# Expert results written by row to a DRAM table and read back once, in place of one-hot products onto the tokens

## The chip, the cores and the metric

The kernel runs on one core of a Trainium2 chip, as one program in one launch. The metric is the device time of one execution in microseconds (us). Times of engines, lines and queues come from a profile of one execution; its own time stands beside the median of the timed runs further down.

## The reference, cut to what matters

Two blocks follow each other on 512 tokens of width 1024, all in float32. The first mixes a bidirectional gated recurrence with a gated spatial mixing; the second has pooling, sparse attention, an attention to 256 memory tokens, and then a mixture of 32 experts in 4 groups of 8. Only the last part is touched. A router picks for each token one group and in it the two best experts, and a weight (gate) for each:

```python
def hierarchical_moe(h, ...):            # h: 512 x 1024, normed
    g_sel = argmax(h @ wg_router + bg_router)            # one of 4 groups
    top_v, top_i = top_k(e_logits of that group, 2)      # two of its 8 experts
    top_w = softmax(top_v) * g_w
    gates = one_hot(g_sel) x (one_hot(top_i) * top_w)
    for g in range(4):
        a = einsum('nd,edf->nef', h, w_gate[g]); b = einsum('nd,edf->nef', h, w_up[g])
        hid = silu(a) * b * gates[:, g, :, None]
        out = out + einsum('nef,efd->nd', hid, w_down[g])
x = x + out
```

So each token receives the results of exactly two experts, 1024 choices in all. An expert has 1 MiB of gate weights, 1 MiB of up weights and 1 MiB of down weights.

## The kernel before

**The stages ahead of the experts.** The kernel first does the two blocks up to the attention to memory. The tokens' values, x, then stand in the tile `fx` (4 tiles of 128 tokens x 1024), and each of the four is also stored to DRAM as `x3d` (L1123). The router works tile by tile (`route`, `count`, `place`): it leaves for each token i and choice j an exact one-hot row over the 32 experts (`ohs`) and the place of the token among those of its expert. An expert has 64 places (`CAP`). Should one expert have more tokens, a loop behind a condition at the end works through the rest; no row of this profile is from it.

**The lists.** `R0` is the one-hot rows times the token's number less 1024 (`tk`, `NOTOK`). `lists_of` (L1213) multiplies it with the one-hot places on TensorE (PE), so that the PSUM tile `plist` holds, for each pair of experts in its column, the token number less 1024 at each of 2 x 64 places, and 0 where a place is empty. `tokens` (L1264) adds 1024 and gives the list as integers (`srci`) and as floats (`srcf`); an empty place gives 1024. `fetch_rows` (L1276) gathers a pair's 128 rows from `x3d` into one of three tiles `hg` with an indirect DMA from GpSimd's queue (POOL); numbers above 511 are left out.

**The loop over the 16 pairs.** Step r works on the experts 2r and 2r+1 together, 64 rows each (L1384). It issues the loads of its gate, up and down weights from SyncE's queue (SP); each goes as soon as its buffer is free, and there are buffers for three pairs (`PLACES`, L1007). `turn_rows` transposes the gathered rows on PE in two groups of four (L1286), `expert_up` scales them on VectorE (L1295), multiplies with gate and up weights in 32 matmuls (`pgu`, L1302), takes Silu on ScalarE (L1306) and the product with the gate on VectorE (L1307). `fetch_rows` for pair r+3 goes out once the rows of pair r are transposed. `expert_down` (L1310) transposes the hidden values (L1316), copies them (L1317), multiplies with the down weights in two halves of 512 columns (`pdn`, 16 matmuls, L1326), and splits each half into a rounded part and a rest (`yh` on ScalarE, L131; `yl` on VectorE, L132), so that a one-hot product keeps the precision.

**Putting the results onto the tokens.** `where` compares the token numbers 0 to 511 with the list on VectorE (L1333) and gives a one-hot matrix `put`, 128 places x 512 tokens. For each of 4 token tiles and 2 halves `add` multiplies it with `yh` (L1339) and `yl` (L1340) and adds the product to `fx` on VectorE (L1341): 16 matmuls and 8 adds per pair. Step r runs this for pair r-1, behind its own up matmuls. The last pair does it at once, and each finished piece of `fx` is stored to `out` (L1357).

**Buffers and order.** Tiles of one tag share a fixed number of buffers, and a new tile waits until an old one of the tag has been read for the last time. The tag `s4` has 8 buffers of 128 x 1024; the tiles `hg`, the scaled rows, `yh` and `yl` use it, and in earlier stages many others. PSUM has three buffers of the tag `mm` (here `pgu`, and half of the products onto the tokens) and three of `sm` (`pdn`, and the other half). Within an engine, instructions run in the order in which the framework's scheduler has put them when the program was built. It does not keep the order of the program text: it takes an instruction when, by its own estimates of durations, what it waits for is done, and among several the one that stands earlier in the text. Semaphores are set by the framework from the tiles that are read and written.

The functions that the diff touches:

Of the kernel before, what the change touches and what calls it, by code (L numbers as in the profile page):

```python
# [4 lines left out]
F32 = mybir.dt.float32  # L5
F32R = mybir.dt.float32r
BF = mybir.dt.bfloat16
I32 = mybir.dt.int32
U8 = mybir.dt.uint8
AF = mybir.ActivationFunctionType  # L10
OP = mybir.AluOpType
# [4 lines left out]
S = 512  # L16
D = 1024
NEG = -3.0e38
GONE = -3.3e38
NOTOK = 1024.0  # L20
# [29 lines left out]
def ap_of(t, off, dims):  # L50

    return bass.AP(tensor=t.tensor, offset=t.offset + off, ap=[t.ap[0]] + [list(d) for d in dims])
# [9 lines left out]
def program(tc, I, out, sb, ps, dr, dbg, upto):  # L62
    nc = tc.nc
# [5 lines left out]
    def c1(shape, name, dt=F32):  # L69
        return sb.tile(shape, dt, name=name)  # L70
# [7 lines left out]
    def s4(name, shape=(128, 2, 512), dt=F32):  # L78
        return sb.tile(list(shape), dt, name=name, tag="s4", bufs=8)
# [80 lines left out]
    def psm(name):  # L160
        return ps.tile([128, 512], F32, name=name, tag="sm", bufs=3)
# [55 lines left out]
    for d in range(2):  # L217
        nc.sync.dma_start(lraw[:, d, :], bass.AP(tensor=lbt.tensor, offset=lbt.offset + d * D,
                                                   ap=[[1, 128], [128, 8]]))
# [231 lines left out]
    for h in range(8):  # L451
        p = ptp(f"tya{h}")
# [48 lines left out]
            split(t, yb[0][:, g, :], yb[1][:, g, :])  # L501


    SC = float(128 ** -0.5)
    mmT = a16("mmT", F32R, (128, 2, 8, 256))
    mw = row_bc(I["mem_norm_2"], D, "mw")
# [13 lines left out]
    mh = rbf[:, 2].rearrange("p (i e) -> p i e", i=4)  # L520
    nc.vector.tensor_scalar(trib, iota, ctok[:, 0:1], None, OP.is_gt)
    nc.gpsimd.memset(oneb, 1.0)
    tk = c1([128, 4], "tk")
    nc.vector.tensor_scalar(tk, ctok, -NOTOK, None, OP.add)
    kvm = e8("kvm", (128, 2, 1024))
    kmT = kvm[:, 0].rearrange("p (h m) -> p h m", h=4)
    vm = kvm[:, 1].rearrange("p (i c) -> p i c", i=2)
# [78 lines left out]
    for ip in range(2):  # L606
        xt = [s4(f"xr{2 * ip + ii}", (128, D)) for ii in range(2)]
        for ii in range(2):
            i = 2 * ip + ii
# [540 lines left out]
    def route(i):  # L1150

        def top(src, k, b, name):

            m8 = sb.tile([128, 8], F32, name=f"{name}8_{i}", tag="m8", bufs=6)
            V_.max(m8, src)
            V_.tensor_copy(best[:, i, b, 0:k], m8[:, 0:k])
            rest = carve(src.shape[-1])
            V_.match_replace(rest, best[:, i, b, :], src, GONE)
            return rest

        gl = lg[:, i, 0:8]
        rest = top(gl, 1, 0, "grp")
        V_.tensor_tensor(rest, rest, gl, OP.is_equal)
        em = carve(32)
        V_.scalar_tensor_tensor(em.rearrange("p (g e) -> p g e", g=4), ap_of(rest, 0, [[1, 4], [0, 8]]), -1e30,
                                ap_of(lg, i * 40 + 8, [[8, 4], [1, 8]]), OP.mult, OP.add)
        rest2 = top(em, 2, 1, "ex")
        V_.tensor_tensor(mh[:, i, :], rest2, em, OP.not_equal)

        def gates():  # L1170
            V_.tensor_copy(best[:, i, 2, 0:1], best[:, i, 1, 0:1])
            rest1 = carve(32)
            V_.match_replace(rest1, best[:, i, 2, :], em, GONE)
            V_.tensor_tensor(ohs[:, 0, i, :], rest1, em, OP.not_equal)
            V_.tensor_tensor(ohs[:, 1, i, :], rest2, rest1, OP.not_equal)
            eg, g = carve(4), carve(4)
            gw, dv, g1, g2 = (g[:, c:c + 1] for c in range(4))
            V_.tensor_scalar(dv, best[:, i, 0, 0:1], -1.0, None, OP.mult)
            nc.scalar.activation(eg, gl[:, 0:4], AF.Exp, bias=dv, accum_out=gw)
            V_.tensor_tensor(dv, best[:, i, 1, 1:2], best[:, i, 1, 0:1], OP.subtract)  # L1180
            nc.scalar.activation(dv, dv, AF.Exp)
            V_.tensor_scalar(g1, dv, 1.0, gw, OP.add, OP.mult)
            V_.reciprocal(g1, g1)
            V_.tensor_tensor(g2, g1, dv, OP.mult)
            V_.tensor_scalar(R0[:, :, i, :], ohs[:, :, i, :], tk[:, i:i + 1], None, OP.mult)
            r = rs[:, i:i + 1]
            for j, gj in enumerate((g1, g2)):
                V_.tensor_scalar(R2[:, j, i, 0, :], ohs[:, j, i, :], gj, r, OP.mult, OP.mult)
            V_.tensor_scalar(R2[:, :, i, 1, :], ohs[:, :, i, :], r, None, OP.mult)
        return gates  # L1190
# [73 lines left out]
    def tokens(p, n, name):  # L1264

        src = sb.tile([128, n], I32, name=name + "_i", tag=name[:2] + "_i")
        V_.tensor_scalar(src, p, NOTOK, None, OP.add)
        e = sb.tile([128, n], F32, name=name + "_e", tag=name[:2] + "_e")
        V_.tensor_scalar(e, p, NOTOK, None, OP.add)
        return src, e  # L1270

    hg = [s4(f"hg{b}", (128, D)) for b in range(3)]
    for b in range(3):
        nc.gpsimd.memset(hg[b], 0.0)
# [32 lines left out]
        V_.scalar_tensor_tensor(sa, sa, gate, pg[:, 256:512], OP.mult, OP.mult)  # L1307
        return sh

    def expert_down(sh, ws, src, name, last=False):  # L1310

        m = 128 // len(ws)
        sa, hd = sh[:, 0:256], sh[:, 256:512].rearrange("p (f t) -> p f t", f=2)
        tp = ptp(f"thd{name}")
        for f in range(2):
            nc.tensor.transpose(tp[:, f * 128:(f + 1) * 128], ap_of(sa, f, [[2, 128]]), ident)  # L1316
        nc.scalar.activation(hd, tp[:, :256].rearrange("p (f t) -> p f t", f=2), AF.Copy)  # L1317
        yh, yl = s4(f"yh{name}", (128, D), F32R), s4(f"yl{name}", (128, D), F32R)
        put = []

        def down(half):
            hs = slice(half * 512, half * 512 + 512)
            po = psm(f"pdn{name}_{half}")
            for f in range(2):
                for a, (gu, dn) in enumerate(ws):
                    nc.tensor.matmul(po[m * a:m * a + m, :], hd[:, f, m * a:m * a + m], dn[f][:, hs],  # L1326
                                     start=f == 0, stop=f == 1)
            split(po, yh[:, hs], yl[:, hs])

        def where():  # L1330
            put.append(w2(f"put{name}", dt=F32R))
            for i in range(4):
                V_.tensor_scalar(put[0][:, i * 128:(i + 1) * 128], iota, float(128 * i), src, OP.add, OP.is_equal)  # L1333

        def add(i, half):
            p = (pmm if half else psm)(f"pad{name}_{i}_{half}")
            hs = slice(half * 512, half * 512 + 512)
            pi = put[0][:, i * 128:(i + 1) * 128]
            nc.tensor.matmul(p, pi, yh[:, hs], start=True, stop=False)  # L1339
            nc.tensor.matmul(p, pi, yl[:, hs], start=False, stop=True)  # L1340
            V_.tensor_tensor(fx[:, i, hs], fx[:, i, hs], p, OP.add)  # L1341

        def add_rows():
            where()
            for i in range(4):
                for half in range(2):
                    add(i, half)

        if last:
            where()  # L1350
            for half in range(2):
                down(half)
            for half in range(2):
                hs = slice(half * 512, half * 512 + 512)
                for i in range(4):
                    add(i, half)
                    nc.sync.dma_start(out[0, i * 128:(i + 1) * 128, hs], fx[:, i, hs])  # L1357
            return None
        for half in range(2):
            down(half)  # L1360
        return add_rows

    srci, srcf = tokens(plist[:, 0:16], 16, "lst")
    for r in range(1, 4):
        fetch_rows(hg[r % 3], srci[:, r:r + 1])
    grs = c1([128, 2, 16], "grs")
# [14 lines left out]
        V_.tensor_copy(nmi, nmx)  # L1381

    add_rows = None
    for r in range(16):  # L1384
        es, (gtags, dtags), last = (2 * r, 2 * r + 1), PLACES[r % 3], r == 15
        gu, fetch = [], []
        for e, tag in zip(es, gtags):
            if e < len(gus):
                gu.append(gus[e])
            else:  # L1390
                t, f = load_gu(e, str(e), tag, True)
                gu.append(t)
                fetch += f
        dn = []
        for x, tag in enumerate(dtags):
            d, f = load_dn(es if len(dtags) == 1 else es[x:x + 1], f"{r}_{x}", tag, True)
            dn += d
            fetch += f
        for f in fetch:
            f()  # L1400
        ws = list(zip(gu, dn))
        rows = turn_rows(hg[r % 3], f"{r}") if r else rows0
        sh = expert_up(rows, grs[:, 1, r:r + 1], grs[:, 0, r:r + 1], ws, f"{r}",
                       None if r else other_lists)
        if r and r + 3 < 16:
            fetch_rows(hg[r % 3], srci[:, r + 3:r + 4])
        if r:
            add_rows()
        add_rows = expert_down(sh, ws, srcf[:, r:r + 1], f"{r}", last)


    nval = nc.values_load(nmi[0:1, 0:1], min_val=0, max_val=S)
# [3 lines left out]
    with tc.If(nval > CAP):  # L1416
        with tc.For_i(0, 32, 1) as e:
# [6 lines left out]
            for j in range(2):  # L1424
                rx = sb.tile([128, 4, 3], F32, name=f"rx{j}v", tag=f"rx{j}")
                for c in range(2):
                    V_.tensor_tensor(t, R2[:, j, :, c, :], ap_of(sel, 0, [[0, 4], [1, 32]]), OP.mult)
                    V_.tensor_reduce(rx[:, :, 1 + c], t, AX.X, OP.add)
                V_.scalar_tensor_tensor(rx[:, :, 0], rx[:, :, 2], 0.0, tk, OP.is_gt, OP.mult)
                Rx.append(rx)  # L1430
            for rr in range(4):
                p = psm(f"plx{rr}")
# [35 lines left out]
```

## Time and profile before

| | us |
|---|---|
| median of 3 runs | 1338.7 (1338.12 to 1342.65) |
| the profiled execution | 1341.01 |
| its span | 1339.2 |
| PE busy | 1300.7 (97%) |
| VectorE (DVE) busy | 776.3 (58%) |
| ScalarE (ACT) busy | 494.1 (37%) |
| GpSimd (POOL) busy | 211.0 (16%) |

The profile shows one execution. The span is the time from its first to its last instruction; the execution's own time is 1.8 us more. PE is the matmuls and PEld the loads of their stationary operand; the ends of matmuls are modelled. L1302 is line 1302 of the kernel. A queue's name has a q behind it (SPq). The granted clock of PE is 1.00 at 2.4 GHz and 0.50 at 1.2 GHz.

### The profile page before, as it was taken

How to read it: one execution, taken by the hardware profiler on the slowest of the kernel's cores; microseconds unless marked ns; L12 is line 12 of the kernel's file. 1: busy time of each engine (PE TensorE's matmuls, PEld its weight loads, DVE VectorE, ACT ScalarE, POOL GpSimd, SP SyncE). 2: the span in 40 equal slices, each digit the busy share in tenths (PEclk: the TensorE clock that was granted, in tenths of full speed). 3: DMA queues.
4: the chain of work that ended last, by engine and by line, in shares of the span. 5: the costliest groups of instructions: out<-in, count | busy, mean ns of one | idle time of the engine just before them, and what ended most of it. 6: DMA issues, size and time to landing. Idle time of an engine off the chain costs nothing. (4 is left out here: it accounts for less than half of the span.)

```text
span 1339.2 us, 21242 instructions
## 1 busy us (share of the span) xinstructions
PE 1300.7 (97%) x8566; PEld 1031.3 (77%) x8566; DVE 776.3 (58%) x1457; ACT 494.1 (37%) x853; POOL 211.0 (16%) x255
## 2 busy tenths in 40 slices
PE   6999999999999999999999999889999999999997
PEld 5898989899988888888899878757898944444443
DVE  4568676666662345444556479993447735555555
ACT  4455464645432244333433334345535211111111
POOL 2203011030010000100012465342011110000000
PEclk9999999999999999999999999899999999999999
DMA  6332223222423433234542322222187579999951
GB/s 187 94 96 62 66 64 95 64 64 64 159 77 95 124 97 92 66 102 158 175 147 68 95 71 64 64 83 95 64 285 297 204 303 417 416 409 414 418 219 65
DMA packets 114454, 207.60 MB, mean 155 GB/s; under 512 B 14342, under 2 KB 93958, under 8 KB 103216
## 3 DMA queue, kind: packets, MB, share of 16 engines
q1 hardware_dynamic: 106096, 197.88, 41.6%
q10 hardware_dynamic: 6096, 4.47, 1.1%
q0 software_dynamic: 2160, 3.85, 0.8%
q8 instruction: 69, 1.13, 0.4%
q14 instruction: 33, 0.27, 0.1%
HBM read 201.81 MB, written 8.39 MB: 157 GB/s over the span
## 5 line engine op out<-in xcount | busy, mean ns | idle before, releaser
L1302 PE MATMUL pgu<-gu,hgT 128*64 128x512 f32 x512 | 113.7, 593 | 0.0
L1302 PEld LDWEIGHTS pgu<-gu,hgT 128*64 128x64 f32 x512 | 37.7, 137 | 71.2 <-issue 66.0
L353 ACT ACTIVATE qk<-G 128x512 f32<-128x512 f32 x112 | 69.1, 665 | 51.6 <-DVE G L343 51.6
L1341 DVE TENSOR_TENSOR fx<-fx,pad 128x512 f32<-128x512 f32 x128 | 77.9, 681 | 1.1 <-PE pad L1340 1.1
L1326 PE MATMUL pdn<-dn,sh 128*64 128x512 f32 x256 | 61.5, 604 | 0.0
L340 DVE TENSOR_TENSOR G<-G,T 128x512 f32<-128x512 f32 x56 | 39.2, 701 | 31.4 <-ACT qk L353 28.6
L1307 DVE SCALAR_TENSOR_TENSOR sh<-sh,grs,pgu 128x256 f32<-128x256 f32 x16 | 7.7, 481 | 80.7 <-ACT sh L1306 80.7
L1339 PE MATMUL pad<-yh,put 128*128 128x512 f32 x128 | 52.8, 416 | 0.9 <-DVE fx L1341 0.9
L1340 PE MATMUL pad<-yl,put 128*128 128x512 f32 x128 | 49.9, 394 | 0.0
L131 ACT ACTIVATE yh<-pdn 128x512 fp32r<-128x512 f32 x32 | 19.1, 597 | 73.8 <-PE pdn L1326 73.8
L1306 ACT ACTIVATE sh<-pgu,grs 128x256 f32<-128x256 f32 x16 | 7.6, 474 | 101.5 <-PE pgu L1302 101.5
L1277 POOL DMA_INDIRECT hg<-x3d,lst_i x15 | 15.1, 1008 | 184.1 <-PE thg L1286 171.3
L304 POOL TENSOR_TENSOR T<-T 128x512 f32<-128x512 f32 (+6 forms) x56 | 37.0, 660 | 42.6 <-DVE T L271 38.8
L153 PE MATMUL pi<-wi,hT_h 128*128 128x256 f32 x128 | 37.7, 295 | 3.3 <-ACT wi L131 1.7
L132 DVE TENSOR_TENSOR yl<-pdn,yh 128x512 fp32r<-128x512 f32 x32 | 22.1, 691 | 31.1 <-ACT yh L131 31.1
L343 DVE TENSOR_TENSOR G<-G,T 128x512 f32<-128x512 f32 x56 | 38.8, 693 | 0.0
L1339 PEld LDWEIGHTS pad<-yh,put 128*128 128x128 f32 x128 | 24.1, 188 | 18.6 <-issue 13.2
L154 PE MATMUL pi<-wi,hT_h 128*128 128x256 f32 x128 | 37.6, 294 | 0.0
L155 PE MATMUL pi<-wi,hT_l 128*128 128x256 f32 x128 | 37.2, 291 | 0.0
L153 PE MATMUL pv<-wv,hT_h 128*128 128x256 f32 x128 | 36.8, 288 | 0.0
L155 PE MATMUL pv<-wv,hT_l 128*128 128x256 f32 x128 | 36.7, 286 | 0.0
L154 PE MATMUL pv<-wv,hT_h 128*128 128x256 f32 x128 | 36.5, 286 | 0.0
(542 smaller groups left out, 4143.3 us busy)
## 6 DMA issues: line engine op xcount, KB each, us to landing
gu<-in_expert_w_gate SPq DMA_DIRECT2D x32, 1024.0 KB, 8.6
gu<-in_expert_w_up SPq DMA_DIRECT2D x32, 1024.0 KB, 13.3
dn<-in_expert_w_down SPq DMA_DIRECT2D x27, 1024.0 KB, 10.2
wo_r<-in_w_out SPq DMA_DIRECT2D x16, 512.0 KB, 3.6
wq_r<-in_w_in SPq DMA_DIRECT2D x12, 512.0 KB, 3.5
dn<-in_expert_w_down SPq DMA_DIRECT2D x10, 512.0 KB, 10.3
wi_r<-in_w_in SPq DMA_DIRECT2D x8, 512.0 KB, 3.6
wfb_r<-in_w_in SPq DMA_DIRECT2D x8, 512.0 KB, 3.6
```

What stands on the lines that cost most here:

```text
L153: nc.tensor.matmul(o, ah, bh, start=first, stop=False)
L154: nc.tensor.matmul(o, ah, bl, start=False, stop=False)
L155: nc.tensor.matmul(o, al, bh, start=False, stop=last)
L304: nc.gpsimd.tensor_tensor(ap_of(T, o, [[n2, 2], [1, n2]]), ap_of(T, a, [[sa, 2], [2, n2]]), ap_of(T, a + 1, [[sa, 2], [2, n2]]), OP.mult)
L340: nc.vector.tensor_tensor(ap_of(G, 0, [[512, 2], [2 * m, nb], [1, m]]), ap_of(G, 0, [[512, 2], [2 * m, nb], [1, m]]), ap_of(T, a + 1, [[sa ...
L343: nc.vector.tensor_tensor(ap_of(G, 1024 + m, [[512, 2], [2 * m, nb], [1, m]]), ap_of(G, 1024 + m, [[512, 2], [2 * m, nb], [1, m]]), ap_of( ...
L353: nc.scalar.activation(ap_of(qk, a * 512, [[2 * m, nb], [m, 2], [1, m]]), ap_of(G, a * 512, [[2 * m, nb], [1024 + m, 2], [1, m]]), AF.Copy)
L1302: nc.tensor.matmul(pg[m * a:m * a + m, :], hT_[:, k, m * a:m * a + m], ap_of(gu, k * 256, [[2048, 2], [1, 256]]), start=k == 0, stop=k == 7)
L1326: nc.tensor.matmul(po[m * a:m * a + m, :], hd[:, f, m * a:m * a + m], dn[f][:, hs], start=f == 0, stop=f == 1)
L1339: nc.tensor.matmul(p, pi, yh[:, hs], start=True, stop=False)
L1340: nc.tensor.matmul(p, pi, yl[:, hs], start=False, stop=True)
L1341: V_.tensor_tensor(fx[:, i, hs], fx[:, i, hs], p, OP.add)
```

## The change

For pairs 0 to 13 (`DIRECT = 14`), the result of a pair is copied out of PSUM as it is, half by ScalarE and half by VectorE, into a tile `yr`, and an indirect DMA from POOL's queue writes its 128 rows into a DRAM table `yd` of 1024 rows: row t for a token's first choice, 512 + t for its second. An empty place has row 1024, which is left out. After pair 13 the table is read back in eight loads of 128 x 1024 on SP's queue, and each is added to `fx` on VectorE. Pairs 14 and 15 are put onto the tokens as before; their rows of the table are not written, so the table is first filled with zeros, from a zeroed tile of tag `s4`, by one DMA of 4 MiB on ScalarE's queue (ACT), issued in the text behind the first block's gated mixing.

The lists now hold the row of the table, and the token is worked out from it: `tk` has a second set of columns with 512 added, `R0` is made in two steps in place of one, and `places` takes the place of `tokens` for the pairs.

```diff
+    yd = dr.tile([2 * S, D], F32, name="yd")
+    zero = s4("zero", (128, D))
+    nc.gpsimd.memset(zero, 0.0)
+    nc.scalar.dma_start(yd.rearrange("(i p) d -> p i d", p=128), ap_of(zero, 0, [[0, 8], [1, D]]))
...
-    tk = c1([128, 4], "tk")
-    nc.vector.tensor_scalar(tk, ctok, -NOTOK, None, OP.add)
+    tk = c1([128, 8], "tk")
+    nc.vector.tensor_scalar(tk[:, 0:4], ctok, -NOTOK, None, OP.add)
+    nc.vector.tensor_scalar(tk[:, 4:8], ctok, S - NOTOK, None, OP.add)
...
-            V_.tensor_scalar(R0[:, :, i, :], ohs[:, :, i, :], tk[:, i:i + 1], None, OP.mult)
+            for j in range(2):
+                V_.tensor_scalar(R0[:, j, i, :], ohs[:, j, i, :], tk[:, 4 * j + i:4 * j + i + 1], None, OP.mult)
...
+    def places(p, n):
+
+        row, rowf = c1([128, n], "row", I32), c1([128, n], "rowf")
+        V_.tensor_scalar(row, p, NOTOK, None, OP.add)
+        V_.tensor_scalar(rowf, p, NOTOK, None, OP.add)
+        src, e = c1([128, n], "srci", I32), c1([128, n], "srcf")
+        V_.tensor_scalar(e, rowf, float(S), -float(S), OP.is_ge, OP.mult)
+        V_.tensor_tensor(e, e, rowf, OP.add)
+        V_.tensor_copy(src, e)
+        return row, src, e
...
-    def expert_down(sh, ws, src, name, last=False):
+    def expert_down(sh, ws, src, name, last=False, row=None):
...
+        if row is not None:
+            yr = s4(f"yr{name}", (128, D))
+            for half in range(2):
+                hs = slice(half * 512, half * 512 + 512)
+                po = psm(f"pdn{name}_{half}")
+                for f in range(2):
+                    for a, (gu, dn) in enumerate(ws):
+                        nc.tensor.matmul(po[m * a:m * a + m, :], hd[:, f, m * a:m * a + m], dn[f][:, hs],
+                                         start=f == 0, stop=f == 1)
+                if half:
+                    V_.tensor_copy(yr[:, hs], po)
+                else:
+                    nc.scalar.activation(yr[:, hs], po, AF.Copy)
+            nc.gpsimd.indirect_dma_start(out=yd, out_offset=bass.IndirectOffsetOnAxis(ap=row, axis=0), in_=yr,
+                                         in_offset=None, bounds_check=2 * S - 1, oob_is_err=False)
+            return None
...
-    srci, srcf = tokens(plist[:, 0:16], 16, "lst")
+    row, srci, srcf = places(plist[:, 0:16], 16)
+
+    def results():
+
+        for i in range(4):
+            for j in range(2):
+                t = s4(f"yt{i}_{j}", (128, D))
+                nc.sync.dma_start(t, yd[j * S + i * 128:j * S + (i + 1) * 128, :])
+                V_.tensor_tensor(fx[:, i, :], fx[:, i, :], t, OP.add)
+
...
+    DIRECT = 14
...
-        if r:
+        if add_rows:
             add_rows()
-        add_rows = expert_down(sh, ws, srcf[:, r:r + 1], f"{r}", last)
+        add_rows = expert_down(sh, ws, srcf[:, r:r + 1], f"{r}", last, row[:, r:r + 1] if r < DIRECT else None)
+        if r == DIRECT - 1:
+            results()
```

## Rows read from the trace of the kernel before

**Rows 1.** The page: busy us and share of each engine; GB/s in 40 slices.
```profile
PE 1300.7 (97%) x8566; PEld 1031.3 (77%) x8566; DVE 776.3 (58%) x1457; ACT 494.1 (37%) x853; POOL 211.0 (16%) x255
...
GB/s 187 94 96 62 66 64 95 64 64 64 159 77 95 124 97 92 66 102 158 175 147 68 95 71 64 64 83 95 64 285 297 204 303 417 416 409 414 418 219 65
```
**Rows 2.** Stretches of 20 us: length, each engine's busy us, clock, DMA share, GB/s.
```profile
1260.00:1280.00 20.00, 20.00 (x96) 9.19 (x96) 11.54 (x23) 2.65 (x5) 0.99 (x1) 1.00 1.02 417
```
**Rows 3.** One period in order of time: start, us, engine, line, operation [idle before].
```profile
1249.14 7.04 PE L1302 MATMUL pgu<-gu,hgT 128*64 128x512 f32 x32
...
1256.11 0.50 PE L1339 MATMUL pad<-yh,put 128*128 128x512 f32 x1
...
1256.25 0.47 ACT L1306 ACTIVATE sh<-pgu,grs 128x256 f32<-128x256 f32 x1 [6.30 <-PE pgu L1302]
...
1259.00 0.39 PE L1316 MATMUL thd<-csq,sh 128*128 128x128 f32 x2
...
1259.59 0.48 PE L1339 MATMUL pad<-yh,put 128*128 128x512 f32 x1
...
1260.69 1.94 PE L1326 MATMUL pdn<-dn,sh 128*64 128x512 f32 x8
...
1264.96 7.04 PE L1302 MATMUL pgu<-gu,hgT 128*64 128x512 f32 x32
```
**Rows 4.** Groups from 960 us on: busy us, mean ns, idle before, releaser.
```profile
L1302 PE MATMUL pgu<-gu,hgT 128*64 128x512 f32 x512 | 113.7, 593 | 0.0
...
L131 ACT ACTIVATE yh<-pdn 128x512 fp32r<-128x512 f32 x32 | 19.1, 597 | 73.8 <-PE pdn L1326 73.8
...
L132 DVE TENSOR_TENSOR wxo<-wxo_r,wxo 128x1024 fp32r<-128x1024 f32 x4 | 4.8, 1220 | 0.3 <-ACT wxo L131 0.3
```
**Rows 5.** DMA from 1100 to 1290: a queue's packets and MB; issues, us to landing.
```profile
q0 software_dynamic: 1584, 2.71, 3.8%
...
hg<-x3d,lst_i POOLq DMA_INDIRECT x11, 8.3
```
**Rows 6.** SP's queue, pair 15's first load, in order of time.
```profile
1272.03 0.33 SPq L979 DMA_DIRECT2D gu<-in_expert_w_gate  x1
```
**Rows 7.** Short stretches, columns as in rows 2.
```profile
999.00:1000.00 1.00, 1.00 (x10) 1.00 (x10) 0.19 (x1) 0.00 (x0) 0.00 (x0) 1.00 1.06 442
...
1086.00:1088.00 2.00, 1.98 (x12) 1.07 (x14) 0.00 (x0) 0.38 (x1) 0.00 (x0) 1.00 0.98 414
...
1290.00:1292.00 2.00, 2.00 (x14) 1.72 (x12) 2.00 (x5) 0.38 (x1) 0.00 (x0) 1.00 0.15 61
```
**Rows 8.** The last two pairs in order of time, columns as in rows 3.
```profile
1304.15 0.48 DVE L1307 SCALAR_TENSOR_TENSOR sh<-sh,grs,pgu 128x256 f32<-128x256 f32 x1 [5.27 <-ACT sh L1306]
...
1312.38 7.04 PE L1302 MATMUL pgu<-gu,hgT 128*64 128x512 f32 x32
...
1323.46 3.65 PE L1326 MATMUL pdn<-dn,sh 128*64 128x512 f32 x16
...
1329.03 4.26 DVE L1341 TENSOR_TENSOR fx<-fx,pad 128x512 f32<-128x512 f32 x7
```
**Rows 9.** Stretches around a wait of PE, columns as in rows 2.
```profile
730.00:735.00 5.00, 2.80 (x21) 2.57 (x21) 5.00 (x11) 0.98 (x2) 2.19 (x3) 0.92 0.00 0
735.00:740.00 5.00, 5.00 (x35) 5.00 (x34) 1.31 (x3) 0.21 (x1) 1.29 (x1) 0.74 0.00 0
```
**Rows 10.** PE in order of time, the first matmul behind that wait.
```profile
733.81 0.77 PE L185 MATMUL tp_h2T_h<-csq,xr 128*128 128x128 f32 x4 [2.20 <-DVE h2T_l L132]
```
**Rows 11.** SP's queue in order of time, four places.
```profile
352.34 0.34 SPq L509 DMA_DIRECT2D mem<-in_mem  x1
...
989.57 3.62 SPq L941 DMA_DIRECT2D x2d<-xs  x2
...
1016.70 0.34 SPq L992 DMA_DIRECT2D dn<-in_expert_w_down  x1
...
1032.83 7.62 SPq L1123 DMA_DIRECT2D x3d<-fx  x2
```

More of the change, by code (lines that the diff above doesn't have):

```diff
@@ L1428, in program @@
                     V_.tensor_reduce(rx[:, :, 1 + c], t, AX.X, OP.add)
-                V_.scalar_tensor_tensor(rx[:, :, 0], rx[:, :, 2], 0.0, tk, OP.is_gt, OP.mult)
+                V_.scalar_tensor_tensor(rx[:, :, 0], rx[:, :, 2], 0.0, tk[:, 0:4], OP.is_gt, OP.mult)
                 Rx.append(rx)
```

## The prediction

> **What bounds the kernel now.** I read the page's first two parts, then the expert stage by stretches, one period of it in order of time, its groups and its DMAs, and then the end. "Pair r" is the step that runs experts 2r and 2r+1.
>
> The reader sees TensorE (PE) at 97% of the span, and late in the span five slices in which the core moves 409 to 418 GB/s [rows 1]. Stretch by stretch it is the same: from 1100 to 1280 us, nine stretches of 20 us, PE is busy 20.00 of 20 us and the DMA share is 1.00 to 1.02 [rows 2]. So two resources are full at once. Which one holds the other? The order of one period tells. The up matmuls of pair 11 start at 1249.14; at 1256.11 PE goes on with 12 matmuls of the write-back (L1339, L1340), with two transposes at 1259.00, four more write-back matmuls from 1259.59, the down matmuls from 1260.69, and the up matmuls of pair 12 at 1264.96 [rows 3]: 15.82 us. The groups show 0.0 idle before the up matmuls [rows 4], so no weights are waited for. The transfers, on the other hand, go out when PE frees a buffer: pair 15's gate and up weights from 1272.03, as the up matmuls of pair 12 end [rows 6]. All weight traffic is over at 1290 + 0.15 x 2 = 1290.3 [rows 7], while pair 15's up matmuls start only at 1312.38 [rows 8]. PE is the bound; weights lie ready more than a pair ahead. The DMA is full at the same time: a period carries 6.29 MB of weights (2 experts x 3 MiB) and a gather of 2.71 MB / 11 = 0.246 MB [rows 5], 6.54 MB, and at 415 GB/s that takes 15.8 us. It has no slack.
>
> **What the change removes.** For pairs 0 to 13: 16 write-back matmuls, 4 compares (L1333), 8 adds to fx (L1341), and of each of two splits the second half. ScalarE stands idle 73.8 us before the 32 splits alone [rows 4], and VectorE is busy 11.54 of 20 us [rows 2]; work saved there is worth nothing by itself. On PE the write-back takes 1259.00 - 1256.11 = 2.9 us and 1260.69 - 1259.59 = 1.1 us. What it covers now comes up: after the up matmuls the hidden values go through Silu (0.47 from 1256.25 on), a product, two transposes (0.39) and a copy before a down matmul can start, four steps of some 0.45 with short gaps, until about 1258.3. Now down starts 4.6 us after up ends; then about 2.2 us, into which the next pair's eight row transposes fit. So PE's own period becomes 15.8 - 2.4 = 13.4 us, at best 15.8 - 4.0 = 11.8 if the next up matmuls fill the gap. 14 pairs x 2.4 = 34 us is what PE alone would give.
>
> **What the DMA lets through.** Not that much, because pair 15's weights can't land earlier: the DMA has been full since 1086 [rows 7]. The end of the weights stays at 1290.3 and is pushed back by what the change adds. Each direct pair writes its rows to yd, as many as it gathered: 0.246 MB, 0.59 us at 417 GB/s. Thirteen such writes lie ahead of the last weights: 7.7 us, and the last weights land at 1298.0. No row shows an indirect write. From below it is 0: with stores of x2d issued among loads [rows 11], one stretch has 442 GB/s [rows 7], above the 417 of the expert stage. From above it is twice as much, if all 128 rows of yr travel: 15.5 us. I take 7.7, since the gather, the nearest row, moved only 60 of its 128 rows (0.246 MB of 4 KB rows).
>
> The Trainium skill ("DMA: Bandwidth & Descriptors", section "Issuing engines are not separate DMA queues") says that transfers from all engines run on the same 16 DMA engines and interleave; this speaks against the change, as POOL's writes take from SP's weights. That page's specifications give a ceiling of 435 GB/s; by it, instead of the 417 measured, the stage's bytes from 1086 on (204 us x 415 GB/s + 3.2 MB = 87.9 MB) would end at about 1288, an estimate from that page, 10 us before mine. The trace shows 415 to 417 held for 180 us, and the measurement decides.
>
> PE's lead, 1312.4 - (1290.3 - 5.0) = 27 us, is used up at 13.4 us per pair against 6.79 MB / 417 = 16.3 us: 27 / 2.9 = 9 pairs. From pair 9 or 10 on the weights set the pace, and PE waits up to 2.9 us per pair. Such a wait costs clock: after 2.20 us of idle before 733.81 [rows 10] the granted clock was 0.92 and 0.74 in the two stretches of 5 us [rows 9], that is 3.4 us at 1.2 instead of 2.4 GHz, 1.7 us of work lost. That fits into the wait until the last pair, where I count 2 us.
>
> **The end.** Pair 15's gate and up weights land one down load (2.1 MB, 5.0 us) before the last: 1293.0, against a use at 1312.38 now. From that use to the end are 26.8 us [rows 8]; with nothing else late the span would be 1293.0 + 26.8 = 1319.8. But what is late next is the reading back. yd's reads wait for pair 13's write: its weights land around 1267, down ends about 1275, and a gather took 8.3 us from issue to landing in this stage [rows 5], so the reads go out at about 1284, on SP, behind all weights issued there before (pair 15's go out as pair 12 ends). 8 x 0.52 MB = 4.2 MB at 417 GB/s: they land from 1299.3 to 1308.1. Each is then added to fx, 128x1024 on VectorE; the nearest rows are 1.22 us (the split of wxo, that shape) [rows 4] and 2 x 0.61 (two adds of 128x512, 4.26 / 7) [rows 8]. The last such add ends at 1309.3. fx is one chain: pair 14's eight adds (4.9 us) come after these, pair 15's after those. PE is held too: pair 14's eight products sit in six PSUM buffers until their adds go, and pair 15's down matmuls need three of the same. I put these at 1309.3 + 6 x 0.61 = 1313.0. From there to the end are 1339.2 - 1323.46 = 15.7 us now [rows 8]: 1328.7. With 2 us for the clock, 1330.7. VectorE's own chain is shorter: 1309.3 + 2 x 4.9 + 1.4 (two splits) + 5.9 (from the last add, 1333.3, to the end) = 1326.4.
>
> **Small edits.** The memset and the 4.2 MB of zeros on ACT's queue need a buffer of tag s4. Loads that stand near them in the program went out as soon as such a buffer came free, mem at 352.34 [rows 11], so the fill falls there: 10 us of DMA beside a chunk of projection weights. If that chunk is late, its split waits on ScalarE, and Silu's and Sigmoid's like behind it in that queue, and then PE for PSUM. Between 0 and 5 us; I take 0, as mem shows that loads there have slack. The three extra VectorE steps in places (0.2 each) delay the first gathers by 0.6 us; the extra steps on tk lie beside PE. A write's issue on POOL is one step more between gathers 15.8 us apart; who waits behind it there is only the next gather, three pairs ahead of its use.
>
> The profiled execution took 1341.0 with a span of 1339.2, and lies 2.3 above the median of 1338.7. A span of 1330.7 is 1330.2 on the median's scale: 1330.
>
> **Rivals.**
> A, read-back hidden: reads or adds don't hold fx, and the end is 26.8 us behind pair 15's weights: 1319.8, on the median 1319. For it: writes might be free; against it: the reads queue behind the weights.
> B, nothing gained: writes cost the upper bound, weights end at 1305.8, and all that follows moves by 7.8: 1338. For it: a DMA that is full already; against it: the gather's 60 rows.
> C, slower, by a wait in VectorE's queue. That engine works in order, and the order is fixed beforehand by the framework's scheduler from its own estimates, not by program order: weights of pair 2 went out at 1016.70, ahead of x3d's stores at 1032.83, which stand before them in the program [rows 11]. If it believes that the reads land soon, their eight adds stand in the queue ahead of pair 14's product L1307, and pairs 14 and 15 wait for them: from that L1307 (1304.15) to the end are 35.0 us [rows 8]; from 1309.3 on that gives 1344. It decides as soon as that L1307 stands behind the last of these adds. Against it: the reads depend on pair 13's last step, which is late by any estimate.
> D, clock: PE, waiting in every pair, stays at 1.2 GHz. Its 13.4 us become 26.8, above 16.3, and from pair 10 on 5 x 10 us are lost: 1370 or more. Against it: 32 up matmuls in a row follow each wait, and after 733.81 the clock came back under such work.
>
> **Numbers.** Forecast 0.42 (its own range 1325 to 1336), A 0.18, B 0.18, C 0.15, D 0.07. This kernel's measurement tells 0.5%, 6.7 us, from no change: below 1332.0 is faster, above 1345.4 slower. Faster: A, and 0.75 of the forecast, 0.50. Slower: D, and C or B with anything late beside them, 0.21. Within: 0.29. The range 1316 to 1347 leaves out D, the late side of C and the early side of A.
>
> **What would show it.** Right: no L1339 before pair 14; DMA share 1.0 to about 1298; from pair 9 or 10 on PE idle before pgu, released by DMA, at some 16.3 us per pair, the granted clock below 1.00 there; eight adds of 128x1024 between 1299 and 1310 with DMA as their releaser. Wrong: no DMA wait before pgu (PE's own period is above 16.3), traffic that ends well off 1298 (the price of a write), reads that land among the weights, or pair 14's product after 1305 behind the new adds (C).

## The result and the profile after

The changed kernel takes 1352.15 us (median of five runs, 1350.01 to 1357.38) against 1338.7 of the kernel before (five runs, 1336.12 to 1342.65): 1.0106 times as long, 95% interval [1.0072, 1.0139]. It is slower by 13 us, where 1330.0 was forecast and 1316 to 1347 allowed. The profiled execution took 1357.1, 5 above its median; its span of 1355.1 is 15.9 us longer than the 1339.2 of before.

Three lines of its page, the engines, the GB/s and POOL's DMA queue (packets, MB), answer [rows 1]:
```profile
PE 1260.5 (93%) x8342; PEld 994.9 (73%) x8342; DVE 700.7 (52%) x1291; ACT 486.0 (36%) x839; POOL 227.8 (17%) x270
...
GB/s 184 94 95 63 64 63 95 63 69 58 267 121 90 97 94 94 89 113 196 145 128 41 119 61 42 94 113 61 83 371 177 240 407 419 417 417 419 416 238 64
...
q0 software_dynamic: 4176, 7.47, 1.5%
```
PE does 40 us less work and yet the span grows. The core moves over 405 GB/s in six slices, in five before. Four stretches, columns as in [rows 2], say where the time lies:
```profile
1100.00:1120.00 20.00, 18.86 (x92) 6.99 (x90) 3.80 (x6) 2.05 (x4) 4.08 (x4) 1.00 1.02 423
...
1260.00:1280.00 20.00, 16.50 (x70) 5.76 (x64) 2.37 (x4) 2.05 (x4) 2.41 (x3) 0.91 1.01 415
1280.00:1300.00 20.00, 1.19 (x8) 0.52 (x4) 0.69 (x1) 0.00 (x0) 1.95 (x2) 0.66 0.82 338
1300.00:1320.00 20.00, 7.41 (x25) 2.91 (x27) 10.91 (x10) 0.00 (x0) 0.00 (x0) 0.57 0.57 218
```
Up to 1280 it is as forecast: DMA share 1.01 to 1.02, PE with gaps (16.50 of 20 us, where [rows 2] had 20.00). Then PE all but stands still for a whole stretch (1.19 of 20 us). The same place in order of time, with POOL's last writes, SP's reads, VectorE and PE:
```profile
1285.52 0.98 POOL L1351 DMA_INDIRECT yd<-yr,row  x1 [7.70 <-DMA yd<-yr,row]
1294.25 0.97 POOL L1351 DMA_INDIRECT yd<-yr,row  x1 [7.75 <-DMA yd<-yr,row]
1302.08 8.80 SPq L1406 DMA_DIRECT2D yt<-yd  x8
1305.74 1.23 DVE L1407 TENSOR_TENSOR fx<-fx,yt 128x1024 f32<-128x1024 f32 x1 [24.46 <-DMA yt<-yd]
...
1309.30 2.51 DVE L1407 TENSOR_TENSOR fx<-fx,yt 128x1024 f32<-128x1024 f32 x2 [0.37 <-DMA yt<-yd]
1311.85 1.29 DVE L1314 TENSOR_TENSOR hgT<-thg,ffc 128x512 f32<-128x512 f32 x2
1312.60 9.31 PE L1321 MATMUL pgu<-gu,hgT 128*64 128x512 f32 x32 [31.41 <-DVE hgT L1314]
1313.06 4.87 DVE L1407 TENSOR_TENSOR fx<-fx,yt 128x1024 f32<-128x1024 f32 x4
...
1322.52 0.48 DVE L1326 SCALAR_TENSOR_TENSOR sh<-sh,grs,pgu 128x256 f32<-128x256 f32 x1 [4.59 <-ACT sh L1325]
```
Read it from the matmuls of 1312.60 upwards. They are pair 14's up matmuls, and they waited 31.41 us for hgT, the turned rows of pair 14. VectorE writes these at 1311.85, right behind four of the eight result adds, and the first of these had waited for the read-back. The reads (L1406) go out at 1302.08, 7.8 us after the last write to yd. Pair 14's product stands at 1322.52, against 1304.15 in [rows 8]: 18.4 later. From there to the end are 32.6 us, 2.4 fewer than the 35.0 of before, since pair 13 has no write-back left behind it. 18.4 - 2.4 = 16.0: the whole loss lies in this one wait and, with 2.3 us, in the slower matmuls behind it (9.31 us against the 7.04 of [rows 3]).

POOL's queue in order of time, gathers (L1296) and writes (L1351), shows why the last write is so late:
```profile
1130.47 1.02 POOL L1296 DMA_INDIRECT hg<-x3d,srci  x1 [11.07 <-PE thg L1305]
1143.87 1.00 POOL L1296 DMA_INDIRECT hg<-x3d,srci  x1 [12.39 <-PE thg L1305]
1157.34 0.98 POOL L1296 DMA_INDIRECT hg<-x3d,srci  x1 [12.46 <-DVE yr L1348]
1158.63 1.02 POOL L1351 DMA_INDIRECT yd<-yr,row  x1 [0.30 <-issue]
...
1248.07 1.00 POOL L1351 DMA_INDIRECT yd<-yr,row  x1 [0.31 <-issue]
1259.46 1.01 POOL L1351 DMA_INDIRECT yd<-yr,row  x1 [10.39 <-DMA yd<-yr,row]
```
Every write goes to the same table, so each waits for the landing of the one before, and where three gathers stand ahead of a write in the queue (1130 to 1158) it also waits for them. Behind the last gather five writes were left over; they go out 8.6 to 11.4 us apart, from 1259.46 to 1294.25, although pair 13's rows were in yr at 1281.3.

### The profile page after: what moved, and what is told of

The parts are those of the page before. It is cut to its first block, busy times and chain, and to the rows that moved or that the text cites. A ratio compares the mean times of both kernels' runs of the same rounds, so it can differ in the third digit from the quotient of the medians.

```text
span 1355.1 us, 20558 instructions
## 1 busy us (share of the span) xinstructions
PE 1260.5 (93%) x8342; PEld 994.9 (73%) x8342; DVE 700.7 (52%) x1291; ACT 486.0 (36%) x839; POOL 227.8 (17%) x270
## 3 DMA queue, kind: packets, MB, share of 16 engines
q0 software_dynamic: 4176, 7.47, 1.5%
## 5 line engine op out<-in xcount | busy, mean ns | idle before, releaser
L1321 PE MATMUL pgu<-gu,hgT 128*64 128x512 f32 x512 | 123.3, 611 | 41.0 <-DVE hgT L1314 36.0
L1345 PE MATMUL pdn<-dn,sh 128*64 128x512 f32 x224 | 51.2, 598 | 0.3
L1296 POOL DMA_INDIRECT hg<-x3d,srci x15 | 15.4, 1028 | 157.7 <-DVE yr L1348 109.5
L1348 DVE COPY yr<-pdn 128x512 f32<-128x512 f32 x14 | 9.7, 692 | 54.3 <-PE pdn L1345 54.3
L154 PE MATMUL pg<-wga,hT_h 128*128 128x256 f32 x128 | 36.5, 285 | 0.0
L153 PE MATMUL pg<-wga,hT_h 128*128 128x256 f32 x128 | 36.4, 285 | 0.0
L155 PE MATMUL pg<-wga,hT_l 128*128 128x256 f32 x128 | 36.2, 283 | 0.0
L1345 PEld LDWEIGHTS pdn<-dn,sh 128*64 128x64 f32 x224 | 14.8, 136 | 27.0 <-issue 24.0
L319 PE MATMUL pl<-qk 128*64 128x64 f32 x896 | 34.3, 225 | 0.0
```

The costliest lines, as they stand in the source:

```text
L153: nc.tensor.matmul(o, ah, bh, start=first, stop=False)
L154: nc.tensor.matmul(o, ah, bl, start=False, stop=False)
L155: nc.tensor.matmul(o, al, bh, start=False, stop=last)
L319: nc.tensor.matmul(p[64 * j:64 * j + 64, c * 64:c * 64 + 64], kt[:, k0:k0 + 64], qt[:, q0:q0 + 64], start=True, stop=True)
L1296: nc.gpsimd.indirect_dma_start(out=h, out_offset=None, in_=x3d, in_offset=bass.IndirectOffsetOnAxis(ap=sidx, axis=0), bounds_check=S - 1, ...
L1321: nc.tensor.matmul(pg[m * a:m * a + m, :], hT_[:, k, m * a:m * a + m], ap_of(gu, k * 256, [[2048, 2], [1, 256]]), start=k == 0, stop=k == 7)
```

## The theories

BUFFERS. yr, yt, hgT, hg, yh and yl come from one set of eight buffers (tag s4). Three hold the gathered rows, and the other five are handed round in program order. There the eight read-back tiles stand ahead of pair 14's turned rows: they take the five buffers, then three of these again, and the turned rows, ninth in the row, get the buffer of the fourth tile, which the fourth add frees. So they wait for the table. (The trace fits: five reads go out from 1302.08 to 1304.7, the other three at 1307.00, 1308.96 and 1310.56, each as one of the first three adds ends, and hgT follows the end of the fourth.) The rivals: ORDER, the adds stand ahead of pair 14 in VectorE's queue by the scheduler's choice alone, which is the prediction's rival C one step earlier; BANDWIDTH, the written bytes take the DMA from the weights; and CHAIN, the loss is that the reads are dated by the row of writes.

## The experiments

**Six pairs instead of 14** (`DIRECT = 6`, read-back behind pair 5).

> Six pairs instead of 14 are written to the table, and the read-back is asked for after pair 5; 3.0 MB instead of 7.2 MB of writes. BUFFERS: pair 6's turned rows wait for the fourth result add in the same way, and these for the read-back behind the last write of the chain: pair 6's up matmuls start near 1193 instead of 1157, the ten pairs left take the 15.8 us of the kernel before, and the time is 1350 to 1368, at 1360: no better than with 14 pairs, although under half is written. BANDWIDTH: the loss goes with the volume written and the gain with the pairs; 1325 to 1335. ORDER: as BUFFERS, since adds and turned rows stand in the same order in VectorE's queue.

Measured: 1364.1 us, ratio 1.0203 [1.0186, 1.0220]. The wait of pair 6, in order of time:
```profile
1174.57 0.97 POOL L1351 DMA_INDIRECT yd<-yr,row  x1 [7.80 <-DMA yd<-yr,row]
1181.88 7.86 SPq L1406 DMA_DIRECT2D yt<-yd  x8
1185.55 3.84 DVE L1407 TENSOR_TENSOR fx<-fx,yt 128x1024 f32<-128x1024 f32 x3 [32.53 <-DMA yt<-yd]
1189.55 1.23 DVE L1407 TENSOR_TENSOR fx<-fx,yt 128x1024 f32<-128x1024 f32 x1
1190.81 1.29 DVE L1314 TENSOR_TENSOR hgT<-thg,ffc 128x512 f32<-128x512 f32 x2
1191.55 8.76 PE L1321 MATMUL pgu<-gu,hgT 128*64 128x512 f32 x32 [38.65 <-DVE hgT L1314]
```
Again four adds, then the turned rows, then the up matmuls, 1.5 us off the expected 1193. (A write moves 0.259 MB, as shown below, so both volumes in the expectation, 3.0 and 7.2 MB, are about twice too high; their proportion stands.) With under half the writes the kernel is slower still: BANDWIDTH is out as the main cause. ORDER isn't yet.

**The adds asked for last**, in the same eight buffers:
```
-        if r == DIRECT - 1:
+        if r == 15:            # ahead of expert_down, behind pair 14's add_rows
             results()
```


> The read-back is asked for in the program after pair 14's results have been put back, in pair 15, in the same eight buffers. BUFFERS: the turned rows of pairs 14 and 15 get their buffers first, up matmuls of pair 14 near 1283 and of pair 15 near 1297; the reads still go out near 1302 because the last write lands then (chain of writes), the adds run from 1306, and with the sixteen put-back adds of pairs 14 and 15 around them VectorE ends near 1330: 1332 us (1327 to 1337). ORDER: the same. BANDWIDTH: above 1342. If the chain of writes is not what dates the reads, they go out near 1290 and the time comes to 1322 to 1326.

Measured: 1332.58 us, 0.9967 [0.9950, 0.9984], the expected figure and a little faster than before. Pair 14's up matmuls start at 1275.78, pair 15's at 1293.14, the reads at 1297.51:
```profile
1275.78 1.07 PE L1321 MATMUL pgu<-gu,hgT 128*64 128x512 f32 x2 [0.75 <-DVE hgT L1314]
...
1293.14 7.55 PE L1321 MATMUL pgu<-gu,hgT 128*64 128x512 f32 x32
...
1297.51 12.80 SPq L1406 DMA_DIRECT2D yt<-yd  x8
```
ORDER allows it too.

**The read-back's own buffers**, asked for ahead of pair 14's work as in the change:
```
-                t = s4(f"yt{i}_{j}", (128, D))
+                t = yts[i // 2][:, 2 * (i % 2) + j, :]    # one tile of tag w16, one of a16
```
(`results()` moves behind the requests for pair 14's weights, so that these keep their buffers.)

> The eight tiles of the read-back are taken from two tiles of other tags (the freed weight buffer of pair 13's down part and one 16 KB weight buffer), no longer from the eight buffers that the row tiles, the turned rows and the result rows share; the reads and adds still stand ahead of pair 14's work in the program. Theory BUFFERS (pair 14's turned rows get the buffer that the fourth result add frees, and so its up matmuls wait for the whole read-back): pair 14's up matmuls start at 1283 +- 3 us instead of 1312.6; its product then stands behind two result adds in VectorE's queue and ends near 1308 instead of 1322, and the run takes 1338 us (1334 to 1343). Rival ORDER (the adds stand ahead of pair 14 in VectorE's queue for their own sake): pair 14's up matmuls still start after 1305 and the time stays within 3 us of 1352. Rival BANDWIDTH (the 7 MB of writes take the DMA engines from the weights, and that is the loss): unchanged within 3 us of 1352, the up matmuls waiting for weights.

Measured: 1350.93 us, 1.0092 [1.0075, 1.0109]: the time of the rivals, with the start of BUFFERS.
```profile
1279.47 1.07 PE L1321 MATMUL pgu<-gu,hgT 128*64 128x512 f32 x2
...
1282.55 8.69 PE L1321 MATMUL pgu<-gu,hgT 128*64 128x512 f32 x30 [2.00 <-DMA gu<-in_expert_w_up]
...
1297.20 1.75 SPq L1407 DMA_DIRECT2D ytw<-yd  x4
...
1301.87 0.44 SPq L986 DMA_DIRECT2D gu<-in_expert_w_gate  x1
...
1321.81 9.54 PE L1321 MATMUL pgu<-gu,hgT 128*64 128x512 f32 x30 [2.99 <-DMA gu<-in_expert_w_up]
```
Pair 14's up matmuls run 30 us earlier (the first two start at 1279.47), but my edit put the reads on SP's queue ahead of pair 15's weights. The queue works in order, the reads waited for the last write until 1297.20, and the weights behind them went out from 1301.87, 27 to 31 us later than in the changed kernel; pair 15's up matmuls wait for them, 30 of the 32 until 1321.81. One wait was exchanged for another, so I took that one away as well: the same kernel with `nc.gpsimd.dma_start` for the reads.

> The run with own buffers for the read-back once more, with the eight reads sent from POOL's queue behind the last write instead of from SP's, where they stood ahead of pair 15's last weights (these went out at 1301.9 to 1306.6 and pair 15's up matmuls waited for them until 1321.8). BUFFERS: pair 14's up matmuls near 1283 again; one or two result adds stand ahead of pair 14's rests, so pair 15's up matmuls start near 1308, the other adds run beside them, and the end comes 26.8 us later: 1336 us (1332 to 1341). Rival ORDER or BANDWIDTH: 1348 or more, as in the run before it.

Measured: 1337.03 us, 0.9989 [0.9973, 1.0006].
```profile
1281.18 7.05 PE L1321 MATMUL pgu<-gu,hgT 128*64 128x512 f32 x30 [1.50 <-DMA gu<-in_expert_w_up]
...
1301.53 2.21 POOL L1407 DMA_DIRECT2D ytw<-yd  x4 [7.29 <-DMA yd<-yr,row]
...
1305.21 1.23 DVE L1408 TENSOR_TENSOR fx<-fx,ytw 128x1024 f32<-128x1024 f32 x1 [15.89 <-DMA ytw<-yd]
1306.35 0.68 DVE L132 TENSOR_TENSOR yl<-pdn,yh 128x512 fp32r<-128x512 f32 x1
1306.95 1.28 DVE L1314 TENSOR_TENSOR hgT<-thg,ffc 128x512 f32<-128x512 f32 x2
1307.69 9.47 PE L1321 MATMUL pgu<-gu,hgT 128*64 128x512 f32 x32 [13.04 <-DVE hgT L1314]
```
The reads go out at 1301.53, as late as in the changed kernel, and pair 14 no longer cares; 1352.15 - 1337.03 = 15.1 us are what the shared buffers cost (15.7 by the two ratios; the move to POOL's queue, which was to undo the wait of the run before, is in it). With other buffers the scheduler itself puts pair 14's turned rows ahead of the adds, although these are still asked for first, so for pair 14 the order was a consequence of the buffers and not the cause. What is left of ORDER is in the last four lines: one result add, which waits for the table, stands ahead of pair 14's last split and pair 15's turned rows, and PE waits 13.04 us.

**Two tables by turns**, the odd pairs' read back and the results of the even pairs left out:
```
-            nc.gpsimd.indirect_dma_start(out=yd, ...
+            nc.gpsimd.indirect_dma_start(out=yds[int(name) % 2], ...
```


> As the changed kernel, but the pairs write by turns into two tables, and only the table of the odd pairs is read back (left out: the results of the even pairs; both tables are filled with zeros first). A write now waits for the write two pairs back. Theory CHAIN (the reads are dated by the writes going one after another, each behind the landing of the one before): the last write goes out soon after its rows are ready at 1281, the reads near 1291 instead of 1302, pair 14's up matmuls start near 1303 instead of 1312.6, and the time is 1343 us (1340 to 1347). Rival (the reads are dated by the weights ahead of them on SP's queue, or by the gathers ahead of the writes on POOL's): reads out at 1298 or later, and the time 1349 to 1353.

Measured: 1355.3 us, 1.0123 [1.0106, 1.0140]. A miss, and not for the rival's reason either.
```profile
1283.74 0.98 POOL L1352 DMA_INDIRECT yd<-yr,row  x1 [17.61 <-DVE yr L1349]
1291.95 17.22 SPq L1407 DMA_DIRECT2D yt<-yd  x8
1305.12 5.05 DVE L1408 TENSOR_TENSOR fx<-fx,yt 128x1024 f32<-128x1024 f32 x4 [22.13 <-DMA yt<-yd]
```
The last write and the reads go out 10 us earlier, as expected. But the first add starts at 1305.12, where it was 1305.74: the reads now run behind the weights still in flight and take 14.2 us to land (median) instead of 5.7. CHAIN dates the reads' issue and is worth nothing here. The likely reason is that the DMA has no room for them until 1300 (share 0.90 to 1.03 in every 2 us from 1290 on); why they need another 5 us after that, no run shows.

**No read-back, and neither read-back nor writes** (`results()` left out; then the write in `expert_down` as well).

> Left out: the eight reads of the table and the eight adds, so the output lacks the results of 14 pairs; all writes stay. BUFFERS: pair 14 waits for nothing late, pair 15's up matmuls start when its weights have landed, near 1297, and the end follows 26.8 us later as in both kernels: 1325.7 us (1321 to 1331), below the kernel before. ORDER says the same. BANDWIDTH: the writes alone hold the weights up, so the time stays above 1342.

> Left out: all writes to the table and its read-back, so the output lacks the results of 14 pairs. Set against the run without read-back alone (1324.8 us) it prices the writes. Pair 15's up matmuls wait there for weights until 1295.5. By the 0.59 us a pair that the prediction charged the weights for a write, 14 writes give 8 us back: 1316.5 us. By the full time of 0.52 MB at 420 GB/s, 1.25 us each, they give 17.5 us back: 1307 us, and TensorE's own 13.4 us a pair (pair 15 at 1276) lies just below. Rival (writes cost the weights nothing, TensorE's clock or the buffers set the pace): within 3 us of 1324.8.

Measured: 1324.76 us, 0.9906 [0.9881, 0.9930], and 1315.24 us, 0.9823 [0.9807, 0.9839]. Pair 15's up matmuls behind the first two, without the read-back:
```profile
1295.54 7.05 PE L1321 MATMUL pgu<-gu,hgT 128*64 128x512 f32 x30 [1.73 <-DMA gu<-in_expert_w_up]
```
and without writes too:
```profile
1285.24 7.05 PE L1321 MATMUL pgu<-gu,hgT 128*64 128x512 f32 x30 [0.51 <-DMA gu<-in_expert_w_up]
```
Both times weights end the wait: the DMA sets this stage's pace. All 14 writes cost 9.5 us, 0.68 each. By the two ratios, each against the kernel before measured beside it, it is 11.1 us, 0.79 each, and the intervals leave some 4 us either way.

**Adds last and own buffers; then ten pairs; then adds on two engines.** The first joins the edits of the second and third experiments, the second sets `DIRECT = 10` in it, the third gives POOL the adds of the last row block:
```
-                V_.tensor_tensor(fx[:, i, :], fx[:, i, :], t, OP.add)
+                (nc.gpsimd if i == 3 else V_).tensor_tensor(fx[:, i, :], fx[:, i, :], t, OP.add)
```


> Adds asked for last, as in the run with 1332.6 us, and the eight tiles of the read-back in the two freed weight buffers, so that no read waits for a buffer. There the eight reads took 12.8 us to go out (from 1297.5), each waiting for a shared buffer, and four of the adds and pair 15's result halves waited behind them. BUFFERS: all eight reads go out within 4 us of the last write's landing at 1297.5, the adds run without a break, VectorE's 21 us of adds after pair 15's product end near 1325, and the time is 1328 us (1325 to 1331). Rival (the adds themselves are the length of the tail, buffers have no part in it): within 2 us of 1332.6.

> As the run before it, with ten pairs written instead of 14; pairs 10 to 14 are put back by products as before. TensorE has 2.4 us a pair to spare against the DMA engines while they set the pace, four writes of 0.52 MB fewer pass them, and the last write lands long before the weights do. Pair 15's up matmuls start near 1292 instead of 1295, the reads go out behind the last weights, and the time is 1325 us (1321 to 1329): below the kernel before by 12 us. If TensorE and not the DMA engines sets the pace at the end, pair 15 starts near 1300 and the time is 1332 or more.

> As the run with 1331.9 us (adds last, own buffers), with the two adds of the last row block on POOL, which stands idle there, instead of VectorE. If VectorE's chain of adds is the length of the tail (it was busy from 1307 to 1322 almost without a break), two adds of 1.22 us leave it and the time is 1329.5 us (1328 to 1331); POOL's own two, at 2.4 us each by its 128x1024 subtractions, end before 1320. If the landing of the reads sets it, within 1 us of 1331.9.

Measured: 1331.94 us, 0.9943 [0.9926, 0.9959]; 1340.72, 1.0010 [0.9995, 1.0025]; 1332.69, 0.9960 [0.9941, 0.9978]. The first is the best version found that computes everything. Its own buffers gained nothing that can be told from adds last alone (1332.58; the intervals overlap), so the expected 1328 was wrong and its rival right: once nothing waits behind the adds, the buffers have no part.

Ten pairs missed the expected time by 16 us. The second case came, PE setting the pace, but by a stall that the expectation did not have. Two lines of VectorE and PE:
```profile
1239.49 1.29 DVE L1314 TENSOR_TENSOR hgT<-thg,ffc 128x512 f32<-128x512 f32 x2 [10.59 <-DMA yd<-yr,row]
1240.23 8.67 PE L1321 MATMUL pgu<-gu,hgT 128*64 128x512 f32 x32 [12.06 <-DVE hgT L1314]
```
Pair 10 is the first to need yh and yl from the eight buffers, while the rows of pairs 7 to 9 still wait to be written (their writes go out at 1229.78, 1240.27 and 1248.92); pair 11's turned rows wait 10.59 us for the first of these. From pair 12 on PE needs its 15.8 us a pair again (up matmuls at 1275.44, 1291.27, 1307.09), and the lost time can't be won back. It is BUFFERS once more, with a write as the holder instead of a read.

## Why the prediction was wrong

**Right: the upstream, PE's period, the bound.** The first up matmuls start at 1075.3 (1076.5 before): the small edits cost nothing that shows, as forecast. (In all twelve traces this start lies between 1071.1 and 1076.5, so one instant of two runs compares only to some us.) Early pairs follow each other every 13.4 us (gathers at 1130.47, 1143.87, 1157.34), the figure forecast. From pair 10 on the DMA is the bound: the up matmuls come 16.2 to 16.8 us apart, 16.3 forecast, and PE waits for weights. Pair 13's:
```profile
1266.21 8.56 PE L1321 MATMUL pgu<-gu,hgT 128*64 128x512 f32 x30 [1.56 <-DMA gu<-in_expert_w_up]
```

**Right within its bounds: the price of a write.** Forecast 0.59 us, bounds 0 and 1.2; measured 0.68, or 0.79 by the ratios. POOL's queue moved 7.47 MB against 3.85 without writes: 0.259 MB a write, 0.62 us at 417 GB/s. Pair 15's gate and up weights were forecast for 1293.0; without the read-back PE waits for them until 1295.54. Rival B, double price, is out. Two slips have no weight: the upper bound was to be all 128 rows, and these, 0.524 MB at 417 GB/s, are 1.26 us a write, 16.3 in all and not 15.5; and of the nine stretches said to have held 415 to 417 GB/s two have 406 and 412. Rival A (1319) is what the run without read-back comes within 6 us of, 1324.76; but that run leaves the adds out, and the best one that has them takes 1331.94.

**Wrong, the step that failed: "The end", what the read-back holds.** The prediction took fx as the one thing that the read-back holds, and looked for PE's hold in PSUM: six product buffers of pair 14. The eight tiles yt it counted as DMA time and as eight adds of VectorE, not as eight requests to the pool from which pair 14's own rows are taken. PE was held a step earlier than any step in the sum, at pair 14's up matmuls, 1312.60, where the sum has pair 15's down matmuls at 1313.0. That is 15.1 us by the run with own buffers. Without it the time is 1337.0; another 5.1 us go when the adds stand behind pair 14's in the program too, and the time is 1331.9 or 1332.6. That this is so near the forecast 1330.0 is in part luck: in the run with 1331.9 us the last result add ends at 1322.8 and pair 15's down matmuls start at 1310.1, where the sum has 1309.3 and 1313.0.

**Wrong in a term, without weight: "the reads go out at about 1284".** They went out at 1302.1. The prediction let pair 13's write go when its rows were ready and forgot 13 writes before it to the same table. But the two tables show that in the changed kernel 10 us on this date moved the first add by 0.6 us.

**Rival C** named the place, pair 14 behind the result adds in VectorE's queue, and had the sign. What the prediction held against it, that the reads are late by any estimate, does not count where a buffer forces the order. Its 1344 was too low: the up matmuls (9.31 us, against 7.04 in [rows 3]) were still to come after the wait, and not just the product.

**The clock.** 2 us were set aside for it. In the two stretches from 1280 the granted clock was 0.66 and 0.57, and pair 14's up matmuls took 2.3 us longer, behind the long wait. It can fall behind a short one too: pair 13's 30 up matmuls in the line above took 8.56 us, against 7.05 to 7.08 in pairs 10 to 12, behind a wait of 1.56 us, and the stretch from 1260 has 0.91. But short waits did not lower it in every pair. Rival D is out: up to 1260 the clock stayed at 1.00.

## What to carry to other kernels

Count a new tile against its pool as you count an instruction against its engine: who holds the buffers when it is asked for, and which later tile gets the one that it frees. A late consumer is harmless only if it is asked for after all that must not wait for it; here that alone turned 1.0106 into 0.9967. The writes to one table went one behind the other here, and the rows that waited for them held buffers too.

## What the runs showed of the hardware

An add on POOL slows VectorE, and the other way round. In the run with adds on two engines POOL took 3.2 us for each of its two (128x1024), and VectorE's adds beside them 2.78 instead of 1.22:
```profile
1309.73 1.21 DVE L1408 TENSOR_TENSOR fx<-fx,ytw 128x1024 f32<-128x1024 f32 x1
1310.87 1.21 DVE L1408 TENSOR_TENSOR fx<-fx,yta 128x1024 f32<-128x1024 f32 x1
1311.14 6.47 POOL L1408 TENSOR_TENSOR fx<-fx,yta 128x1024 f32<-128x1024 f32 x2 [18.91 <-DMA yta<-yd]
...
1312.60 2.78 DVE L1408 TENSOR_TENSOR fx<-fx,ytw 128x1024 f32<-128x1024 f32 x1
1315.31 0.68 DVE L132 TENSOR_TENSOR yl<-pdn,yh 128x512 fp32r<-128x512 f32 x1
1315.90 2.78 DVE L1408 TENSOR_TENSOR fx<-fx,ytw 128x1024 f32<-128x1024 f32 x1
```
Two adds taken off VectorE saved 2.4 us there, and two others lost 3.1; so the exchange had nothing to gain (1329.5 us expected, 1332.7 measured). The split, with one of its two sources in PSUM, kept its 0.68. The Trainium skill ("SBUF — State Buffer", section "SBUF: two separate sides") says that VectorE and GpSimd share a pair of ports as a lock, and that of a VectorE operation with two SBUF inputs and a GpSimd operation that reads SBUF the one that starts first holds it to its end. This trace agrees: POOL's two adds end at 1314.30 and 1317.61, and VectorE's slow ones 1.08 and 1.07 us behind them, at 1315.38 and 1318.68; POOL's end 2.22 and 2.23 us behind the VectorE adds that end at 1312.08 and 1315.38. So the adds of the two engines went one after the other, VectorE's at about its own 1.22; a lone add on POOL no run has.

A write of a 128-row tile moved 0.259 MB, half of its 0.524: 1024 choices over 16 pairs are 64 rows a pair, 0.262 MB, so of the rows without a token nothing went over the queue, as with the gathers [rows 5].
